# One joint inversion for both streams, mixers without GpSimd, and longer runs of part-array products in a two-layer hybrid transformer

## The chip, the core and the metric

The kernel runs on one core of a Trainium2 chip. The metric is the device time of one execution in microseconds (us), the median of the runs shown. The core has a matrix engine (TensorE, in the profile PE; its weight loads are PEld), two engines for elementwise work (VectorE, DVE; ScalarE, ACT), GpSimd (POOL), and SyncE (SP), which issues every transfer here. TensorE writes to PSUM, eight banks of 128 x 512 fp32; all else lies in SBUF.

## The reference

Two layers over two streams of 256 tokens of width 1024: the context `c` and the image `x`. Each layer has a mixer with three branches (a gated delta rule with 8 heads in two directions, a chunk MLP, a pooling branch), then an expert layer of 16 experts in which each expert chooses its tokens. In the second layer the context gives only its states.

```python
def gated_delta_chunked(q, k, v, g, beta, s0):
    ...
    m = jnp.where(strict, jnp.einsum('nbhik,nbhjk->nbhij', kb, kc) * decay, 0.0)
    a = m + jnp.eye(C, dtype=m.dtype)
    rhs = jnp.concatenate([vc * bc[..., None], kb * jnp.exp(gc)[..., None]], axis=-1)
    sol = lax.linalg.triangular_solve(a, rhs, left_side=True, lower=True, unit_diagonal=True)
    ...
    def step(s, xs):
        v_new = u_ - jnp.einsum('bhck,bhkv->bhcv', w_, s)
        o_ = (jnp.einsum('bhck,bhkv->bhcv', q_ * jnp.exp(g_)[..., None], s)
              + jnp.einsum('bhij,bhjv->bhiv', at_, v_new))
        ...
        s = (s * jnp.exp(g_last)[..., None]
             + jnp.einsum('bhck,bhcv->bhkv', k_ * jnp.exp(g_last - g_)[..., None], v_new))
...
for l in range(DEPTH):
    ctx_mix, ctx_states = hybrid_mixer(hc, zero_states, 1, lp, states_only=last)
    x_mix, _ = hybrid_mixer(hx, ctx_states, ROWS, lp, states_only=False)
    x = x + g1x * x_mix
    ...
    x = x + g2x * expert_choice_ffn(hx2, lp)
    ...
```

## The kernel before

The program is recorded first and ordered later. `Net` writes down each operation through `Prog.record`; `Prog.order` is a list scheduler with a cost for each operation (`Prog.cost`) that picks, engine by engine, the next operation by priority (the place where it was recorded, plus a bias) among those whose inputs are ready; `Prog.emit` then issues that fixed order, so every instruction of the profile has the line L623. `s.any`, `s.av`, `s.vg` and `s.ad` stand for operations that the scheduler may give to one of several engines.

Projections multiply in split single precision: each weight tile is cut into a high and a low part (`wsplit`: a ScalarE copy, then a subtraction), and each product is three fp32r products. The gated delta rule works on 128-token chunks, two per stream, and two heads at a time (`j` counts the four head pairs). For each stream and head pair `heads_in` projects, convolves and normalizes keys, values and queries; `heads_solve` makes the triangular matrices `MT` (two chunks x two directions x two heads = 8 of 128 x 128) from transferred rows of decays and calls `inverse`; `heads_scan` carries the state through the chunks; `heads_out` normalizes and gates. The other branches (`side`: `chunk_mlp`, `pooling`, gates) are a generator from which `gdn` takes pieces between these steps; what is left runs behind them. Then come `merge` (branches joined, output projection), `route` (which expert takes which token) and `moe`, in which 16 x 12 tiles of 1 MB of expert weights are loaded for each layer.

`inverse` inverts the 32 x 32 diagonal blocks in four doubling levels. A level is a set of 32 x 32 products into bank `P`, a masked copy `Pn` by VectorE (two halves), a second set into bank `Qm`, an addition and a 32 x 32 block transpose by VectorE. Two more steps join blocks to 64 (`P32`, `Y32`) and to 128 (`P64`, `Y64`). There are 64 small instructions in a set (8 matrices x 4 blocks, each fp32 product being two instructions). One call for each stream and head pair: 8 calls in a layer.

In `Prog.order` ready 32 x 32 products (`op.tile`) wait in a queue of their own beside that of all other TensorE work. The scheduler stays with the small ones only while they write the same bank and the count is no multiple of `quad=12`:

```python
if ready[e] and (x < ready[e][0] and not much or ops[x[1]].a[0].tile is group[0] and group[1] % s.limits["quad"]):
    queues.reverse()
```

In the mixers GpSimd takes the elementwise products of `heads_solve` (`E`, `Eb`, `qt`), the decay of the state in `heads_scan`, most of `heads_out`, the weighting in `heads_z`, parts of `chunk_mlp`, and, where the scheduler chooses it, subtractions and additions of `wsplit`, `split_x`, `side` and `merge`.

Of the kernel before, what the change touches and what calls it, by code (L numbers as in the profile page):

```python
# [5 lines left out]
F32 = mybir.dt.float32  # L6
# [96 lines left out]
def _layouts(inp):  # L103
# [14 lines left out]
    o["gnw"] = f(g["gdn_norm_w"])  # L118
# [103 lines left out]
class Op:  # L222
    __slots__ = ("i", "eng", "fn", "a", "k", "tiles", "deps", "succ", "nd", "cost", "ready", "start", "end", "on", "prio", "gate", "inst", "win", "tile", "fill")
# [34 lines left out]
class Prog:  # L258
    def __init__(s, nc, pool, banks, limits):
# [6 lines left out]
        s.any = Eng(s, ("act", "dve", "pool"))  # L266
        s.av, s.vg = Eng(s, ("act", "dve")), Eng(s, ("dve", "pool"))
# [13 lines left out]
    def record(s, eng, fn, a, k):  # L281
# [47 lines left out]
        op.tile, op.fill = False, 1.0  # L329
# [6 lines left out]
    def cost(s, op, acc):  # L336
# [16 lines left out]
        if op.eng[0] == "pe":  # L353
            if op.fn == "transpose":
                return {"pe": n * 2 / 2.4 + 2}
            m = acc[0][0].shape[0]
            op.fill = min(m, 128) * acc[1][0].shape[0] / 16384
# [15 lines left out]
    def order(s):  # L373
# [110 lines left out]
        recent, group = [], [None, 0]  # L484
# [21 lines left out]
        while left:  # L506
# [17 lines left out]
            for e in engines:  # L524
# [3 lines left out]
                if e == "pe":  # L528
# [3 lines left out]
                    if ready["tile"]:  # L532
# [5 lines left out]
                        if ready[e] and (x < ready[e][0] and not much or ops[x[1]].a[0].tile is group[0] and group[1] % s.limits["quad"]):  # L538
                            queues.reverse()
                aside, tries = [], 0  # L540
                while queues:
# [26 lines left out]
                    if e == "pe":  # L568
                        if not span[3]:
                            c *= 2  # L570
                        if group[0] is not None and not op.tile:
                            c += 80.0
                        group[1] = group[1] + 1 if op.tile and op.a[0].tile is group[0] else 1
                        group[0] = op.a[0].tile if op.tile else None
                        span[1] += c * op.fill
                        span[2] += c
                        if not op.tile:
                            recent.append((now, c * op.fill))
# [52 lines left out]
POOLW = (0, 6)  # L631
# [5 lines left out]
FILL = (3, 1, 1)  # L637
ROOM = dict(w=0, wa=0)
EVERY = (0.7, 1.0)
NY = 3  # L640
# [12 lines left out]
class Net:  # L653
# [43 lines left out]
    def run(s):  # L697
        tc, t = s.tc, s.t
        limits = dict(w=4, hi=5, wa=5, we=18, fill=0.94, window=800, spare=0, clock=4096 / 1.2, share=0.5, quad=12, room=ROOM)
# [9 lines left out]
    def record(s):  # L709
# [28 lines left out]
        for n, sh in (("n1", [128, 2, 8]), ("conv", [128, 2, 24, 5]), ("psc", [128, 2, 4]), ("wr", [128, 2, 8, 16]),  # L738
                      ("alog", [128, 2, 16]), ("dtb", [128, 2, 16]), ("gnw", [128, 2, 128])):
# [15 lines left out]
        for n in ("conv", "psc", "wr"):  # L755
            nc.sync.dma_start(s.small[n], t[n])
        for n, w in (("alog", 16), ("dtb", 16), ("gnw", 128)):
# [59 lines left out]
    def ada(s, l, parts):  # L817

        nc, t = s.nc, s.t
        for g, halves in parts:  # L820
            ps = s.bank("ada")
            js = [j for a in halves for j in (2 * a, 2 * a + 1)]
            for kt in range(8):
                ws = {}
                for a in halves:
                    w = s.p.tile([128, 2, 512], F32, name="wada", lim="wa")
                    nc.sync.dma_start(w.rearrange("p a b -> p (a b)"), t["w_ada"][l, g, a, kt])
                    ws[a] = w
                if kt == 0:
# [4 lines left out]
                for j in js:  # L834
                    s.mm(ps[32 * j:32 * j + 32, :], s.cs32[:, kt, :], ws[j // 2][:, j % 2, :], False, kt == 7)
# [60 lines left out]
    def wsplit(s, src):  # L896
# [14 lines left out]
        s.tt(lo, w, hi.bitcast(F32), ALU.subtract, s.p.vg if s.wn > POOLW[s.l] else nc.gpsimd)  # L911
# [52 lines left out]
    def gdn(s, l, ms, side):  # L964
        p = s.p
        Y, X = [], []
        for r in range(NY):
            Y.append(p.tile([128, 2, 2, 2, 128], F32, name="Y"))
            s.nc.gpsimd.memset(Y[r], 0.0)
            X.append(p.tile([128, 2, 2, 64], F32, name="X64"))  # L970
            s.nc.gpsimd.memset(X[r], 0.0)
        c, x = ms
        slot = lambda m, j: (Y[(2 * j + m.k) % NY], X[(2 * j + m.k) % NY])
        full = [m for m in ms if m.full]
        qkv, sol, zs = {}, {}, {}
# [13 lines left out]
        for m in ms:  # L989
# [857 lines left out]
```

## Time and profile before

| what | value |
|---|---|
| time, median of 3 runs | 2430.93 us (2430.82 to 2431.25) |
| time of the profiled execution | 2433.34 us |
| its span, first to last instruction | 2431.6 us |
| mean granted TensorE clock | 0.961 |
| TensorE, VectorE, ScalarE, GpSimd busy | 2118.4, 1172.9, 647.9, 370.6 us |
| moved from HBM | 597.58 MB |

The span falls into two mixers (to about 883 us, and from 1338 to about 1970 us) and two expert stages behind them. "Busy" counts an instruction from its start to its modelled end, and those of TensorE overlap, so the pace of TensorE is better read from how many instructions a stretch holds. A stretch counts every instruction that touches it, those of its neighbours at both ends too.

### The profile page before, as it was taken

The numbers are of one execution on the slowest core, as the hardware profiler recorded it, in microseconds if no ns is written. First come the engines' busy times: TensorE is split into PE (matmuls) and PEld (weight loads), VectorE is DVE, ScalarE is ACT, GpSimd is POOL, SyncE is SP. The second block draws the span as 40 slices with busy tenths as digits, with TensorE's granted clock in tenths as the row PEclk, the third lists the DMA queues.
The fourth block names the chain that finished last, engine by engine and source line by source line (L and its number), as shares of the span: only waits on it lengthen the run. The fifth ranks groups of instructions, "written<-read, shape, count | busy, mean of one in ns | idle before, by whom it ended". The sixth has DMA issues, their size and how long they took to land.

```text
span 2431.6 us, 50016 instructions
## 1 busy us (share of the span) xinstructions
PE 2118.4 (87%) x21357; PEld 1351.6 (56%) x21357; DVE 1172.9 (48%) x2712; ACT 647.9 (27%) x1329; POOL 370.6 (15%) x334
## 2 busy tenths in 40 slices
PE   8999999999999999878787899999899977676665
PEld 4777867787779842222222477777789931111211
DVE  4978776854326831212121797788765531010102
ACT  4534343323224520000000454344434420000000
POOL 0233332510000410000000212232330010000000
PEclk9999999999999999999999999999899988888888
DMA  8432333323346689999999634333236879999997
GB/s 291 146 101 82 117 90 99 99 102 101 118 162 203 214 320 421 421 421 421 421 421 421 243 113 152 128 118 122 69 101 217 317 315 421 421 421 421 422 421 307
DMA packets 153910, 603.11 MB, mean 248 GB/s; under 512 B 13820, under 2 KB 60092, under 8 KB 104536
## 3 DMA queue, kind: packets, MB, share of 16 engines
q1 hardware_dynamic: 153688, 599.93, 64.9%
q8 instruction: 167, 2.74, 0.4%
q14 instruction: 55, 0.45, 0.1%
HBM read 597.58 MB, written 2.29 MB: 247 GB/s over the span
## 4 chain that ended last, share of the span: by engine, by line
PE 45%; DMA 36%; DVE 12%; issue 3%; POOL 2%; ACT 1%; SPq 0%; DVEq 0%; ACTq 0%; POOLq 0%
PE bank L623 45%; DMA page<-in_w_up_dram 22%; DVE page L623 12%; DMA page<-in_w_down_dram 12%; POOL page L623 2%; ACT page L623 1%; DMA page<-in_w_gate_dram 0%; DMA page<-in_n_dram 0%; DMA page<-in_b_ada_dram 0%; DMA page<-rows 0%; SPq L623 0%; DMA page<-in_w_ada_dram 0%; DVEq L1843 0%; DVEq L623 0%; POOLq L623 0%
## 5 line engine op out<-in xcount | busy, mean ns | idle before, releaser
L623 PE MATMUL bank<-page,page 32*32 32x32 f32 (+8 forms) x18473 | 2074.4, 335 | 299.6 <-DVE page L623 107.3
L623 PEld LDWEIGHTS bank<-page,page 128*128 128x128 f32 (+5 forms) x18473 | 1300.2, 144 | 1048.4 <-issue 381.3
L623 POOL TENSOR_TENSOR page<-page,page 128x512 f32<-128x512 f32 (+4 forms) x277 | 313.5, 1146 | 1444.1 <-DVE page L623 1050.3
L623 ACT ACTIVATE page<-page 128x1024 fp32r<-128x1024 f32 (+8 forms) x462 | 326.5, 721 | 534.2 <-PE bank L623 273.6
L623 ACT ACTIVATE page<-bank 128x512 f32<-128x512 f32 (+5 forms) x341 | 164.9, 501 | 1106.9 <-PE bank L623 1012.1
L623 DVE TENSOR_TENSOR page<-page,page 128x1024 fp32r<-128x1024 f32 (+6 forms) x389 | 338.5, 888 | 118.9 <-ACT page L623 102.0
L623 DVE TENSOR_TENSOR page<-page,bank 128x256 f32<-128x256 f32 (+2 forms) x184 | 101.4, 558 | 575.9 <-ACT page L623 269.1
L623 DVE TENSOR_TENSOR page<-bank,page 128x128 f32<-128x128 f32 (+4 forms) x350 | 154.5, 460 | 287.2 <-PE bank L623 282.6
L623 ACT ACTIVATE page<-page,page 128x128 f32<-128x128 f32 (+2 forms) x319 | 119.9, 435 | 50.2 <-POOL page L623 31.2
L623 DVE COPY page<-bank 32x128 f32<-32x128 f32 (+7 forms) x175 | 71.4, 408 | 60.9 <-PE bank L623 58.9
L623 DVE SCALAR_TENSOR_TENSOR page<-page,page,page 128x508 f32<-128x508 f32 (+3 forms) x128 | 94.5, 757 | 1.2
L623 DVE SCALAR_TENSOR_TENSOR page<-page,page 128x508 f32<-128x508 f32 (+5 forms) x115 | 75.9, 665 | 14.1 <-DMA page<-in_n_dram 11.7
L623 PE MATMUL bank<-page 32*32 32x32 f32 (+1 forms) x2884 | 76.2, 204 | 2.8 <-DVE page L623 2.4
L623 PEld LDWEIGHTS bank<-page 32*32 32x32 f32 (+1 forms) x2884 | 59.2, 114 | 20.0 <-issue 8.5
L623 POOL MEMSET page<- 128x1024 f32 (+2 forms) x13 | 7.6, 630 | 398.6 <-DMA page<-in_w_up_dram 389.7
L623 DVE TENSOR_SCALAR page<-page 128x4 f32<-128x4 f32 (+7 forms) x215 | 52.6, 258 | 26.2 <-ACT page L623 19.2
L623 DVE STREAM_TRANSPOSE page<-page 32x32 f32<-32x32 f32 (+1 forms) x208 | 57.8, 288 | 4.2
L623 DVE SCALAR_TENSOR_TENSOR page<-page,bank 128x512 f32<-128x512 f32 x48 | 32.7, 684 | 55.9 <-PE bank L623 54.7
L623 ACT ACTIVATE page<-bank,page 128x128 f32<-128x128 f32 (+2 forms) x81 | 36.7, 483 | 78.5 <-PE bank L623 60.0
L623 DVE TENSOR_TENSOR page<-page 128x4 f32<-128x4 f32 (+3 forms) x252 | 50.5, 209 | 4.1
L623 POOL TENSOR_TENSOR page<-page 128x512 f32<-128x512 f32 x22 | 30.9, 1406 | 138.7 <-DVE page L623 96.1
L623 DVE TENSOR_SCALAR page<-page,page 128x128 f32<-128x128 f32 (+3 forms) x125 | 47.4, 416 | 5.2 <-ACT page L623 4.8
(25 smaller groups left out, 235.5 us busy)
## 6 DMA issues: line engine op xcount, KB each, us to landing
page<-in_w_gate_dram SPq DMA_DIRECT2D x128, 1024.0 KB, 19.8
page<-in_w_up_dram SPq DMA_DIRECT2D x128, 1024.0 KB, 19.8
page<-in_w_down_dram SPq DMA_DIRECT2D x128, 1024.0 KB, 19.8
page<-in_w_in_dram SPq DMA_DIRECT2D x136, 512.0 KB, 3.6
page<-in_w_ada_dram SPq DMA_DIRECT2D x96, 512.0 KB, 4.6
page<-rows SPq DMA_DIRECT2D x88, 256.0 KB, 5.0
page<-in_w_br_a_dram SPq DMA_DIRECT2D x24, 512.0 KB, 4.7
page<-in_w_out_dram SPq DMA_DIRECT2D x24, 512.0 KB, 4.6
```

The lines of the kernel that those rows point to most:

```text
L623: op.inst = getattr(eng[op.on], fn)(*a, **k)
```

## The change

- **Joint inversion.** `heads_solve` now takes both streams: `products` fills the `MT` of each (two tiles, one for each direction, of 8 matrices), and one call of `inverse` handles all 16. A set has 128 small instructions in a full bank; VectorE works on 512 columns at once instead of 256, with one masked copy instead of two halves. 4 calls in a layer. Two slots for the results instead of three; the order in `gdn` and the pieces taken (`FILL`) follow.
- **No GpSimd in the mixers.** Its operations go to VectorE, some to ScalarE (squares with accumulation in `heads_out`; the state's decay to either). Two products of `heads_out` become one instruction for each head, and the norm weight moves into the ScalarE copy behind the transposes. `route`, `final` and the zeroing of buffers keep GpSimd.
- **Longer runs.** Every product with at most 64 rows or columns (`op.part`) waits in the small queue, those of the experts and of `ada` too, and once the scheduler has begun with one it stays until none is ready. Its prices change with it. `ada` issues the products of two weight tiles together.

```diff
@@ Prog.cost
-            op.tile = m <= 32 and acc[1][0].shape[0] <= 32
+            op.tile = m <= 32 and k <= 32
+            op.part = m <= 64 or k <= 64
             if acc[2][0].dtype == F32R and n >= 256:
-                return {"pe": n / 2.4 + 2}
-            c = max(n, m) / 1.2 * 2 + 4
-            return {"pe": c if m > 64 else c * (0.6 if m > 32 else 0.25) + 20 if n < 128 else c * (0.5 if m > 32 else 0.25) + 14}
+                return {"pe": n / 2.4 + 13.5}
+            c = n / 0.6 + 10
+            if op.tile:
+                return {"pe": 9.0}
+            if op.part:
+                return {"pe": max(c / (4 if m <= 32 or k <= 32 else 2) + 6, 30)}
+            return {"pe": max(c, 223)}
@@ Prog.order
-                        heapq.heappush(ready["tile" if op.tile else e], (op.prio, op.i))
+                        heapq.heappush(ready["tile" if op.part else e], (op.prio, op.i))
...
-                        if ready[e] and (x < ready[e][0] and not much or ops[x[1]].a[0].tile is group[0] and group[1] % s.limits["quad"]):
+                        if ready[e] and (x < ready[e][0] and not much or group[2]):
                             queues.reverse()
...
-                        if group[0] is not None and not op.tile:
-                            c += 80.0
+                        if group[2] and not op.part:
+                            c += 225.0
+                        elif op.part and not group[2]:
+                            c += 95.0
+                        group[2] = op.part
...
-POOLW = (0, 6)
-FILL = (3, 1, 1)
-NY = 3
+FILL = (6, 1, 2)
+NY = 2
@@ ada
-            for kt in range(8):
+            for k2 in range(4):
...
+                for kt in (2 * k2, 2 * k2 + 1):
+                    for j in js:
+                        s.mm(ps[32 * j:32 * j + 32, :], s.cs32[:, kt, :], ws[kt, j // 2][:, j % 2, :], False, kt == 7)
@@ wsplit
-        s.tt(lo, w, hi.bitcast(F32), ALU.subtract, s.p.vg if s.wn > POOLW[s.l] else nc.gpsimd)
+        s.tt(lo, w, hi.bitcast(F32), ALU.subtract)
@@ gdn
-        for m in ms:
-            sol[m.k] = s.heads_solve(m, 0, qkv[0][m.k], slot(m, 0))
-            take(FILL[0])
+        sol = s.heads_solve(ms, 0, qkv[0], Y[0], X[0])
+        take(FILL[0])
...
-                o[m.k], S = s.heads_scan(m, j, qkv[j][m.k], sol[m.k], S)
+                o[m.k], S = s.heads_scan(m, j, qkv[j][m.k], now[m.k], S)
                 take(FILL[1])
-                if j < 3:
-                    sol[m.k] = s.heads_solve(m, j + 1, qkv[j + 1][m.k], slot(m, j + 1))
+                if j < 3 and m is ms[0]:
+                    sol = s.heads_solve(ms, j + 1, qkv[j + 1], Y[(j + 1) % NY], X[(j + 1) % NY])
                     take(FILL[2])
@@ heads_solve
+    def heads_solve(s, ms, j, qkv, Y, XF):
+        MT = [s.p.tile([128, 8, 128], F32, name="MT") for d in range(2)]
+        part = {m.k: s.products(m, j, qkv[m.k], [a[:, 4 * z:4 * z + 4, :] for a in MT]) for z, m in enumerate(ms)}
+        s.inverse(MT, Y, XF)
+        return {m.k: (Y[:, :, 4 * z:4 * z + 4, :],) + part[m.k] for z, m in enumerate(ms)}
+    def products(s, m, j, qkv, MT):
...
-            s.tt(E, R[0], s.nb[:, :, None, :].to_broadcast(B4), ALU.add, G)
+            s.tt(E, R[0], s.nb[:, :, None, :].to_broadcast(B4), ALU.add)
...
-            s.tt(Eb, E, R[2], ALU.mult, G)
-            s.tt(MT[:, i], kq[:, 0][:, None].to_broadcast(B4), Eb, ALU.mult)
+            s.tt(Eb, E, R[2], ALU.mult)
+            for d in range(2):
+                s.tt(MT[d][:, 2 * i:2 * i + 2, :], kq[:, 0], Eb[:, d], ALU.mult)
...
@@ heads_scan
-                    s.tt(sd[:, d], S[:, d], col(i, 5)[:, d, :, None].to_broadcast([128, 2, 128]), ALU.mult, G)
+                    for h in range(2):
+                        s.p.ad.scale(sd[:, d, h, :], S[:, d, h, :], col(i, 5)[:, d, h:h + 1])
@@ heads_out
-        s.tt(osq, o, o, ALU.mult, G)
-        V.reduce_sum(so, osq, axis=AX.X)
+                s.act(s.p.tile([128, 128], F32, name="osq"), o[:, i, h, :], AF.Square, accum_out=so[:, i, h:h + 1])
...
-        s.tt(o, o, ro[:, :, :, None].to_broadcast(B4), ALU.mult, G)
-        s.tt(o, o, zs, ALU.mult, G)
+                V.scalar_tensor_tensor(o[:, i, h, :], o[:, i, h, :], ro[:, i, h:h + 1], zs[:, i, h, :], op0=ALU.mult, op1=ALU.mult)
...
@@ inverse
-        C5 = [128, 2, 2, 2, 32]
+        C4 = [128, 2, 8, 32]
...
-            for (i, d, h) in units:
+            for (d, u) in units:
                 for q in range(4):
-                    s.mm(pp[Q[q], i, d, h, :], MT[Q[q], i, d, h, 32 * q:32 * q + 32], X[Q[q], i, d, h, :], True, True)
-            for i in range(2):
-                s.tt(Pn[:, i], pp[:, i], s.nm[:, lv, :, None, :].to_broadcast([128, 2, 2, 32]), ALU.mult)
+                    s.mm(pp[Q[q], d, u, :], MT[d][Q[q], u, 32 * q:32 * q + 32], X[Q[q], d, u, :], True, True)
+            s.tt(Pn, pp, s.nm[:, lv, :, None, :].to_broadcast(C4), ALU.mult)
...
-        for i in range(2):
-            for h in range(2):
-                V.transpose(XF[Q[1], i, h, 0:32], Y[Q[0], i, 0, h, 32:64])
-                V.transpose(XF[Q[2], i, h, 32:64], Y[Q[3], i, 1, h, 64:96])
+        V.transpose(line(XF[Q[1], 0]), line(yc[Q[0]]))
+        V.transpose(line(XF[Q[2], 1]), line(yc[Q[3]]))
...
@@ merge
-            s.tt(x[:, :, cs], x[:, :, cs], tm, ALU.add, s.p.vg if c < 3 else V)
+            s.tt(x[:, :, cs], x[:, :, cs], tm, ALU.add)
```

## Rows read from the trace of the kernel before

**Rows 1.** The page, busy us (share of the span) and instructions of each engine.
```profile
PE 2118.4 (87%) x21357; PEld 1351.6 (56%) x21357; DVE 1172.9 (48%) x2712; ACT 647.9 (27%) x1329; POOL 370.6 (15%) x334
```

**Rows 2.** Windows by stage: length, busy PE, PEld, DVE, ACT, POOL, clock, DMA share, GB/s.
```profile
90.00:510.00 420.00, 395.10 (x6649) 315.34 (x6649) 318.32 (x817) 163.09 (x383) 148.15 (x136) 0.98 0.32 99
510.00:780.00 270.00, 269.88 (x1614) 217.58 (x1600) 117.24 (x180) 84.10 (x114) 16.36 (x15) 1.00 0.40 135
...
883.00:1338.00 455.00, 388.06 (x1634) 121.60 (x1632) 81.58 (x119) 12.99 (x20) 6.43 (x9) 1.00 1.01 416
1338.00:1440.00 102.00, 91.83 (x579) 59.59 (x580) 83.25 (x220) 51.68 (x119) 23.22 (x14) 0.95 0.55 196
1440.00:1797.00 357.00, 330.23 (x6288) 263.10 (x6287) 280.94 (x751) 155.76 (x365) 112.81 (x110) 0.97 0.37 116
1797.00:1925.00 128.00, 128.00 (x1110) 126.99 (x1109) 77.58 (x106) 53.45 (x63) 5.59 (x4) 1.00 0.62 207
...
1970.00:2431.60 461.60, 309.01 (x2157) 90.26 (x2155) 62.45 (x130) 15.65 (x28) 4.98 (x4) 0.87 0.97 402
```

**Rows 3.** The chain that ended last, in order of time: start us, us, what.
```profile
516.35 263.47 PE bank L623 x1436
...
998.75 19.81 DMA page<-in_w_down_dram
```

**Rows 4.** Windows of TensorE alone: length, busy PE (instructions that touch it), clock, DMA.
```profile
108.19:108.87 0.68, 0.68 (x64) 1.00 0.00 0
...
242.07:242.62 0.55, 0.55 (x49) 1.00 0.90 209
242.62:243.17 0.55, 0.55 (x11) 1.00 0.78 276
243.17:243.43 0.26, 0.26 (x18) 1.00 0.91 331
1840.00:1860.00 20.00, 20.00 (x169) 1.00 0.64 192
1802.17:1802.78 0.61, 0.61 (x17) 1.00 0.11 27
```

**Rows 5.** Lines by form of TensorE, 242.08 to 242.61 and 242.63 to 243.16 us.
```profile
L623 PE MATMUL bank<-page,page 32*32 32x32 f32 x48 | 0.6, 195 | 0.0
...
L623 PE MATMUL bank<-page,page 128*128 128x256 f32 x3 | 0.6, 314 | 0.0
```

**Rows 6.** Lines by form of TensorE, 90 to 880 and 1340 to 1965 us: its 32 x 32 products.
```profile
L623 PE MATMUL bank<-page,page 32*32 32x32 f32 x3328 | 46.3, 196 | 13.5 <-DVE page L623 8.2 <-issue 5.1
L623 PE MATMUL bank<-page 32*32 32x32 f32 x1280 | 19.0, 197 | 2.8 <-DVE page L623 2.4 <-issue 0.4
...
L623 PE MATMUL bank<-page,page 32*32 32x32 f32 x3200 | 45.9, 196 | 15.2 <-DVE page L623 9.3 <-issue 5.9
```

**Rows 7.** Lines by form of GpSimd and VectorE: whole span, then 1880 to 1920 and 90 to 510 us.
```profile
L623 POOL TENSOR_TENSOR page<-page,page 128x512 f32<-128x512 f32 x144 | 196.1, 1372 | 1145.3 <-DVE page L623 924.3 <-PE bank L623 81.3 <-DMA page<-rows 79.5
L623 DVE TENSOR_TENSOR page<-page,page 128x512 f32<-128x512 f32 x33 | 23.3, 706 | 1.0
L623 DVE TENSOR_TENSOR page<-bank,page 128x512 f32<-128x512 f32 x74 | 49.5, 685 | 30.9 <-PE bank L623 29.0 <-POOL page L623 0.9 <-ACT page L623 0.4
L623 DVE TENSOR_TENSOR page<-bank,page 128x128 f32<-128x128 f32 x128 | 31.4, 283 | 30.1 <-PE bank L623 29.9
L623 DVE TENSOR_TENSOR page<-page,bank 128x256 f32<-128x256 f32 x88 | 35.8, 417 | 62.3 <-PE bank L623 62.1
L623 DVE STREAM_TRANSPOSE page<-page 128x256 f32<-128x256 f32 x80 | 35.2, 440 | 1.2
...
L623 DVE TENSOR_TENSOR page<-page,page 128x1024 fp32r<-128x1024 f32 x13 | 15.7, 1221 | 3.3 <-ACT page L623 3.3
L623 DVE TENSOR_TENSOR page<-page,page 128x1024 fp32r<-128x1024 f32 x31 | 41.8, 1351 | 7.2 <-ACT page L623 6.8
```

**Rows 8.** The chain that ended last, 780 to 890 us: shares of the stretch by line.
```profile
by line: PE bank L623 47.8%; DVE page L623 25.4%; DMA page<-in_n_dram 7.4%; POOL page L623 7.2%; issue 6.7%; DMA page<-in_w_ada_dram 4.1%; ACT page L623 1.6%; DVEq L623 0.1%; POOLq L623 0.1%
```

More of the change, by code (lines that the diff above doesn't have):

```diff
@@ L222 @@
 class Op:
-    __slots__ = ("i", "eng", "fn", "a", "k", "tiles", "deps", "succ", "nd", "cost", "ready", "start", "end", "on", "prio", "gate", "inst", "win", "tile", "fill")
+    __slots__ = ("i", "eng", "fn", "a", "k", "tiles", "deps", "succ", "nd", "cost", "ready", "start", "end", "on", "prio", "gate", "inst", "win", "tile", "part", "fill")
 class Eng:
@@ L328, in record @@
             op.win = 10 ** 9
-        op.tile, op.fill = False, 1.0
+        op.tile, op.part, op.fill = False, False, 1.0
         op.cost = s.cost(op, shapes)
@@ L698, in run @@
         tc, t = s.tc, s.t
-        limits = dict(w=4, hi=5, wa=5, we=18, fill=0.94, window=800, spare=0, clock=4096 / 1.2, share=0.5, quad=12, room=ROOM)
+        limits = dict(w=4, hi=5, wa=5, we=18, fill=0.94, window=800, spare=0, clock=4096 / 1.2, share=0.5, room=ROOM)
         with tc.tile_pool(name="sb", bufs=1) as sb, tc.tile_pool(name="ps", bufs=1, space=PSUM) as ps, \
@@ L1272, in heads_scan @@
         nc, k, full, cl = s.nc, m.k, m.full, m.cl
-        V, G = nc.vector, nc.gpsimd
+        V = nc.vector
         B4 = [128, 2, 2, 128]
@@ L1363, in heads_out @@
         s.rsqrt(ro, so, [2, 2])
-        s.tt(o, o, ro[:, :, :, None].to_broadcast(B4), ALU.mult, G)
-        s.tt(o, o, zs, ALU.mult, G)
+        for i in range(2):
+            for h in range(2):
+                V.scalar_tensor_tensor(o[:, i, h, :], o[:, i, h, :], ro[:, i, h:h + 1], zs[:, i, h, :], op0=ALU.mult, op1=ALU.mult)
         yp = s.bank("yp").rearrange("p (h c) -> p h c", h=2)
@@ L1384, in inverse, with c4 @@
-        units = [(i, d, h) for i in range(2) for d in range(2) for h in range(2)]
-        YT = s.p.tile(C5, F32, name="Yc")
+        flat = lambda a: a.rearrange("p d u c -> p (d u c)")
+        units = [(d, u) for d in range(2) for u in range(8)]
+        def c4(name):
+            return s.bank(name).rearrange("p (d u c) -> p d u c", d=2, u=8)
+        YT = s.p.tile(C4, F32, name="Yc")
         for q in range(4):
             for d in range(2):
-                s.tt(YT[Q[q], :, d], MT[Q[q], :, d, :, 32 * q:32 * q + 32],
-                     s.nm[Q[q], 0, 1 - d, None, None, :].to_broadcast([32, 2, 2, 32]), ALU.mult, s.p.vg)
@@ L1411, in inverse @@
+            V.transpose(flat(YT), flat(X))
         for q in range(4):
-            for d in range(2):
-                s.p.any.copy(Y[Q[q], :, d, :, 32 * q:32 * q + 32], YT[Q[q], :, d, :, :])
-        s.p.any.copy(XF[Q[0], :, :, 0:32], X[Q[0], :, 0])
-        s.p.any.copy(XF[Q[1], :, :, 32:64], X[Q[1], :, 0])
-        s.p.any.copy(XF[Q[2], :, :, 0:32], X[Q[2], :, 1])
-        s.p.any.copy(XF[Q[3], :, :, 32:64], X[Q[3], :, 1])
-        th = [(i, h) for i in range(2) for h in range(2)]
-        c3 = lambda name, w: s.bank(name)[:, 0:4 * w].rearrange("p (t h c) -> p t h c", t=2, h=2)
+            s.p.av.copy(units16(Y)[Q[q], :, 32 * q:32 * q + 32], units16(YT)[Q[q]])
@@ L1421, in inverse @@
+        for q in range(4):
+            s.p.av.copy(XF[Q[q], q % 2], X[Q[q], q // 2])
+        c3 = lambda name, w: s.bank(name)[:, 0:8 * w].rearrange("p (u c) -> p u c", u=8)
         pp = c3("P32", 32)
-        for (i, h) in th:
+        for u in range(8):
             for a, b in ((0, 1), (2, 3)):
-                s.mm(pp[Q[b], i, h, :], MT[Q[a], i, 0, h, 32 * b:32 * b + 32], X[Q[a], i, 0, h, :], True, True)
-                s.mm(pp[Q[a], i, h, :], MT[Q[b], i, 1, h, 32 * a:32 * a + 32], X[Q[b], i, 1, h, :], True, True)
```

148 lines of the change are left out of this document (71 added, 77 removed).

## The prediction, made before the changed kernel was run

> **What bounds the kernel now.** I read the page's busy times first, then windows cut by stage, then the chain that ended last, then short windows inside the inversions. The page puts TensorE at 87% of the span [rows 1], but that is an average over stages of two kinds. In the two expert stages DMA is at its limit: 416 GB/s with a DMA share of 1.01 from 883 to 1338 us, and 402 GB/s in the last 462 us [rows 2], where the chain goes from transfer to transfer at 19.8 us a step [rows 3]. The change moves no byte of these, and TensorE has 67 of 455 us free in the first of them, so they only start earlier or later. What can move is the mixers. There TensorE is busy 395 of 420 and 330 of 357 us while the gated delta rule runs, and without a gap in the stretches behind it (270 and 128 us), when only side branches are left [rows 2, 3]. With work left over at the end, a mixer's length is TensorE's own time plus its gaps, not the latency of an inversion. So each edit is priced by what it takes from TensorE's issue or adds to its gaps.
>
> **What a change of shape costs TensorE.** In the windows, a run of 48 small (32 x 32) instructions takes 0.55 us to the start of the next wide one, a run of 16 takes 0.26 us (the counts beside them hold one and two wide ones still in flight) [rows 4, 5]. The slope is 0.29/32 = 0.009 us for each, and 0.55 - 48 x 0.009 = 0.115 us is left for going in and out. Between them stand 3 products of 128 x 256, in 0.55 us [rows 4, 5]; undisturbed, 168 of them take 20 us (a count of 169 with one in flight), 0.119 us each [rows 4], so 0.55 - 0.36 = 0.19 us is lost on the wide side. One excursion costs 0.115 + 0.19 = 0.31 us, whatever its length.
>
> **How many there are.** Read in this way, the inversions make 291 runs of small products in the two mixers (142 and 149), the first at 108.19 us with 64 instructions, the last at 1802.17 us [rows 4]. By the code 16 calls with 12 sets each are 192; the rest are sets cut at 24 products (48 instructions) by the limit of 12, as in 48 + 16 above.
>
> **The change part by part.**
>
> *Joint inversion and longer runs.* The products are the same in number: 4608 small instructions in the first mixer [rows 6], 128 in a set now instead of 64, at the same 0.009 us. Only excursions go. Eight calls with 12 uncut sets are 96 runs, 195 fewer: 195 x 0.31 = 60 us. The least I can argue for is what half of it would be, each joint set broken in two by a late operand: 192 runs, 99 fewer, 31 us. The most adds other part products that join an inversion's run; I put 10 us on that, some 30 more excursions.
>
> *`ada` in pairs.* 32 steps become 16 pairs, 16 excursions fewer, 16 x 0.31 = 5 us at most, 0 if the queue had joined them already; I take 4.
>
> *Gaps at the hand-overs.* TensorE stands idle 13.5 + 2.8 + 15.2 = 31.5 us before small products [rows 6]. There are half as many hand-overs now, each longer: a level's VectorE work for two calls was 2 x (2 x 0.283 + 0.417 + 0.440) = 2.8 us, and is about 0.685 + 0.685 + 0.7 = 2.1 us in one (the transpose of 512 columns estimated from that of 256 and the ratio 685 to 417) [rows 7]. But two calls could cover one another before. Halved gaps would be -16 us, all of them gone -31 us, doubled gaps +31 us. I take 0, in the middle, and keep both ends.
>
> *GpSimd's work to VectorE.* A 128 x 512 product takes GpSimd 1.37 us and VectorE 0.71 us [rows 7], a ratio of 0.51. In the two stages with inversions GpSimd's 148 and 113 us thus become at most 76 and 58 us; some vanish (norm weight, one of two passes in `heads_out`) or go to ScalarE, which is busy 163 of 420 us [rows 2]. Against that stand 0.77 us saved at each of 16 levels in a mixer, 12 us. VectorE also loses time when GpSimd works beside it: its subtraction of 128 x 1024 averages 1.35 us between 90 and 510 us, and 1.22 us where GpSimd stands still [rows 7], 4 us for 31 of them, and other forms with two SBUF inputs should gain in the same way. VectorE then has at most 318 + 76 - 12 - 4 = 378 of 420 and 281 + 58 - 12 = 327 of 357 us. That is under the bound, and wide products cover what waits, so I charge TensorE nothing. Without that cover it would cost what VectorE exceeds its stage by, priced below.
>
> *Latencies with no cover.* From 780 to 890 us, where the branches merge and tokens are routed, the chain runs over GpSimd for 7.2% of 110 us, 8 us [rows 8]. At the ratio above most of it falls to half: 4 us gained. At the start of a layer the joint call must wait for both streams' matrices, and from 1338 to 1440 us VectorE is already busy 83 of 102 us with 23 us of GpSimd's work to come [rows 2], 12 us at the ratio. TensorE has projections to do there. Value taken 0, bound 12 us lost.
>
> *Nothing for the rest.* Two slots instead of three, the small load of the norm weight and the zeroed buffers are hidden behind projections. Expert products in the small queue may run ahead of transposes, but DMA sets that stage's pace and 67 us of TensorE are free in it [rows 2].
>
> **The sum.** -60 - 4 - 4 = -68 us. The profiled execution took 2433.3 us, 2.4 us over the median of the runs, so 2433.3 - 68 = 2365.3 us for it, and 2430.9 - 68 = 2363 us as a median.
>
> **A rule that speaks against it.** The granted clock is 0.98 and 0.97 in the two stages with inversions [rows 2]; at two levels, 2.4 and 1.2 GHz, that is 2 x (0.02 x 420 + 0.03 x 357) = 38 us at the lower one. The stages behind them, nearly without small products, stand at 1.00 [rows 2]. The Trainium skill, in "TensorE: Matmul & The Clock Gate", section "What's actually happening", says that the throttled state is the default and that the matrix engine's activity releases it. By that rule longer runs that fill a sixteenth of the array could lower the clock more often; by the rows the present runs cost little. It becomes a rival below.
>
> **The rivals.**
> 1. *The runs fall by half only.* Joint sets break where a bank or operand is late. For it: sets are cut already. Against it: one masked copy now frees a whole set at once. 2430.9 - 31 - 4 - 4 = 2392 us.
> 2. *The joint call is not covered (slower).* One chain instead of two that interleave: VectorE's part of it is about 4 x 2.1 us in the levels and, estimated from the same rows, 11 us around them, 20 us a call, 160 us for 8. Today 31.5 us of hand-overs are bare. The gain of 68 us is gone when 100 of the 160 us are bare, 62%; at 75% it is 120 - 31.5 - 68 = +20, 2451 us. Against it: the wide work left behind both stages, 270 and 128 us [rows 2], is available as cover.
> 3. *VectorE becomes the bound (slower).* If GpSimd's work took as long on VectorE as before, it would need 318 + 148 = 466 of 420 and 281 + 113 = 394 of 357 us, 83 us too much: 2430.9 - 68 + 83 = 2446 us. The ratio of 0.51 speaks against it.
> 4. *The clock falls more often.* Twice the 38 us at the lower level, half of them lost: +19, 2382 us.
>
> **How the numbers follow.** Forecast 0.62, rival 1 0.17, rival 2 0.11, rival 3 0.05, rival 4 0.05. The predicted time is 2363 us. The forecast's own range takes the bounds of its unknown terms: -31 and -10 below, 2322; +31 above, 2394. To hold 8 in 10 it must reach beyond rival 1 with some of its gaps, and towards the slower cases without holding them: 2318 to 2425 us. Faster by over 0.2% (4.9 us, about what a measurement of this kernel can tell from no change) 0.82; within 0.2% 0.04, from the passage between rivals 1 and 2; slower 0.14.
>
> **What would show it.** Right: wide and small runs alternate about 100 times in the two mixers for the inversions, with runs of 128; the stages behind them keep TensorE without a gap; the expert stages keep their 455 us and start earlier by what the mixers lost; idle time before small products stays near 31 us; VectorE's 128 x 1024 subtraction falls to 1.22 us everywhere; GpSimd is idle in the mixers. Wrong: idle before small products over 100 us (rival 2), VectorE above 95% in the stages with inversions (rival 3), a granted clock under 0.95 there (rival 4), or some 190 runs (rival 1). It would also be wrong if the new prices in the scheduler moved the wide work itself, which I priced at nothing.

## The result, and the profile after

The changed kernel takes 2394.73 us (median of 4 runs, 2393.57 to 2398.76) against 2431.07 us for the kernel before on the same chip: a ratio of 0.985, with a 95% interval of 0.984 to 0.987. That is 36 us faster, where 68 us were forecast, and inside the range of 2318 to 2425 us. The profiled execution took 2393.84 us. Its page, with each engine's busy time in us (share of the span) and number of instructions:

```profile
span 2392.1 us, 49338 instructions
PE 2041.2 (85%) x21357; PEld 1344.3 (56%) x21357; DVE 1122.6 (47%) x2478; ACT 686.3 (29%) x1466; POOL 49.3 (2%) x41
```

TensorE has the same 21357 instructions as in [rows 1] and is busy 77 us less. GpSimd's 370.6 us are down to 49.3, and VectorE, which took most of that work over, is busy *less* than before: 1122.6 us against 1172.9. The windows by stage of the changed kernel (length, busy PE, PEld, DVE, ACT, POOL, clock, DMA share, GB/s):

```profile
90.00:497.00 407.00, 369.91 (x6813) 309.33 (x6811) 302.67 (x733) 180.54 (x437) 0.00 (x0) 0.97 0.31 97
497.00:757.00 260.00, 259.51 (x1444) 219.24 (x1443) 110.93 (x170) 86.71 (x128) 0.00 (x0) 1.00 0.44 149
...
866.00:1317.00 451.00, 385.36 (x1636) 123.03 (x1636) 82.73 (x120) 12.99 (x20) 8.64 (x8) 1.00 1.01 418
...
1420.00:1754.00 334.00, 290.19 (x6334) 250.69 (x6320) 238.33 (x558) 159.91 (x398) 0.00 (x0) 0.93 0.32 102
1754.00:1908.00 154.00, 154.00 (x1292) 153.84 (x1291) 96.44 (x146) 70.53 (x104) 0.00 (x0) 1.00 0.69 237
```

Against [rows 2]: the first expert stage keeps its pace at a DMA share of 1.01, and the side stages stay without a gap. But the stages with inversions have 37 and 44 us without TensorE at work, where the kernel before had 25 and 27, and the granted clock is 0.97 and 0.93 there, where it was 0.98 and 0.97. The last expert load of each layer leaves 20.5 and 38.5 us earlier (1307.8 and 2355.0 us against 1328.3 and 2393.5), so each mixer gave about 20 us, where some 34 were expected. The 32 x 32 products by form, 90 to 860 us and then 1318 to 1945 us (busy us, mean ns of one | idle before them, and what ended it):

```profile
L628 PE MATMUL bank<-page,page 32*32 32x32 f32 x4416 | 53.8, 200 | 24.4 <-issue 24.0 <-DVE page L628 0.3
L628 PE MATMUL bank<-page 32*32 32x32 f32 x192 | 2.3, 194 | 1.2 <-issue 1.2
...
L628 PE MATMUL bank<-page,page 32*32 32x32 f32 x4224 | 50.6, 200 | 23.7 <-issue 22.9 <-DVE page L628 0.7
L628 PE MATMUL bank<-page 32*32 32x32 f32 x384 | 4.8, 208 | 0.5 <-issue 0.5
```

The sum, 49.8 us, stands against 31.5 us in [rows 6]. More telling is the releaser: before it was mostly VectorE, now it is "issue", time in which TensorE waits for nothing that the profile shows. TensorE's timeline at 228 us (start, length, what, [idle before]) shows where these gaps lie, and the DMA view of 225 to 262 us what else goes on:

```profile
227.81 2.43 PE L628 MATMUL bank<-page,page 32*32 32x32 f32 x94
231.09 2.74 PE L628 MATMUL bank<-page,page 32*32 32x32 f32 x128 [0.85 <-issue]
235.10 1.97 PE L628 MATMUL bank<-page,page 32*32 32x32 f32 x50 [1.26 <-issue]
236.99 0.87 PE L628 MATMUL bank<-page 32*32 32x32 f32 x78
239.10 0.64 PE L628 MATMUL bank<-page 32*32 32x32 f32 x50 [1.24 <-issue]
```
```profile
GB/s 0 0 0 0 186 337 62 0 18 0 0 0 18 0 0 0 18 0 0 0 18 0 0 0 97 257 221 9 18 0 0 18 0 0 0 18 0 0 0 0
...
q8 instruction: 9, 0.15, 1.6%
```

The gaps stand in the middle of a burst, 0.85 to 1.26 us each. Between the larger transfers, a small one comes every 3 to 4 us (the lone 18s of the GB/s line): the instruction queue, with 9 packets of 16 KB in 37 us. Over the whole span it moves 167 of them, for 2 x 21357 matmuls and weight loads: 256 instructions a packet. A joint set of 64 products is 128 matmuls and 128 weight loads, 256 instructions in some 1.2 us.

In the table below, *runs* are TensorE's runs of products on part of the array in the two mixers (those of `ada` and of other small work too, so 361 where the prediction counted 291 of the inversions alone), *inside* is its idle time within stretches of 32 x 32 products, and *idle* all its idle time from 85 us to the first expert products of each layer, all summed from the trace's matmuls in order.

### The profile page after: what moved, and what is told of

Its sections match the earlier page's. It is cut to its first block, busy times and chain, and to the rows that moved or that the text cites. A ratio compares the mean times of both kernels' runs of the same rounds, so it can differ in the third digit from the quotient of the medians.

```text
span 2392.1 us, 49338 instructions
## 1 busy us (share of the span) xinstructions
PE 2041.2 (85%) x21357; PEld 1344.3 (56%) x21357; DVE 1122.6 (47%) x2478; ACT 686.3 (29%) x1466; POOL 49.3 (2%) x41
## 4 chain that ended last, share of the span: by engine, by line
PE 49%; DMA 36%; DVE 9%; issue 4%; ACT 2%; SPq 0%; DVEq 0%; ACTq 0%
PE bank L628 49%; DMA page<-in_w_up_dram 19%; DMA page<-in_w_down_dram 10%; DVE page L628 9%; DMA page<-in_w_gate_dram 3%; ACT page L628 2%; DMA page<-in_w_in_dram 1%; DMA page<-rows 1%; DMA page<-in_w_ada_dram 1%; DMA page<-in_n_dram 0%; SPq L628 0%; DMA page<-in_b_ada_dram 0%; ACT L628 0%; DVEq L1849 0%; DVEq L628 0%
## 5 line engine op out<-in xcount | busy, mean ns | idle before, releaser
L628 PE MATMUL bank<-page,page 32*32 32x32 f32 (+8 forms) x20611 | 2024.4, 322 | 338.0 <-DVE page L628 99.0
L628 PEld LDWEIGHTS bank<-page,page 32*32 32x32 f32 (+5 forms) x20611 | 1321.4, 143 | 1031.5 <-issue 398.8
L628 ACT ACTIVATE page<-page 128x1024 fp32r<-128x1024 f32 (+7 forms) x485 | 341.4, 719 | 499.3 <-PE bank L628 244.7
L628 DVE TENSOR_TENSOR page<-page,page 128x1024 fp32r<-128x1024 f32 (+3 forms) x471 | 401.5, 876 | 151.7 <-ACT page L628 128.4
L628 DVE TENSOR_TENSOR page<-page,bank 128x512 f32<-128x512 f32 (+2 forms) x152 | 96.6, 644 | 578.8 <-ACT page L628 265.7
L628 DVE TENSOR_TENSOR page<-bank,page 128x512 f32<-128x512 f32 (+4 forms) x286 | 147.7, 530 | 283.8 <-PE bank L628 280.5
L628 ACT ACTIVATE page<-page,page 128x128 f32<-128x128 f32 (+2 forms) x388 | 143.9, 435 | 48.4 <-DVE page L628 41.0
L628 DVE SCALAR_TENSOR_TENSOR page<-page,page,page 128x508 f32<-128x508 f32 (+4 forms) x188 | 107.8, 595 | 1.2
L628 DVE COPY page<-bank 128x512 f32<-128x512 f32 (+7 forms) x100 | 52.6, 527 | 36.9 <-PE bank L628 35.4
L628 DVE SCALAR_TENSOR_TENSOR page<-page,page 128x512 f32<-128x512 f32 (+5 forms) x93 | 65.2, 706 | 9.5 <-DMA page<-in_n_dram 7.4
L628 ACT ACTIVATE page<-bank,page 128x256 f32<-128x256 f32 (+2 forms) x85 | 42.0, 516 | 83.3 <-PE bank L628 64.7
```

Of the source, the lines that this page charges most:

```text
L628: op.inst = getattr(eng[op.on], fn)(*a, **k)
```

## The experiments

Every ratio is to the kernel before on the same chip.

| kernel | us | ratio, 95% interval | runs | inside, us | idle, us |
|---|---|---|---|---|---|
| before | 2431.1 | | 361 | 11.0 | 85.4 |
| changed | 2394.7 | 0.985 (0.984 to 0.987) | 139 | 46.9 | 117.1 |
| x1_cut32 | 2401.8 | 0.989 (0.987 to 0.991) | 198 | 25.9 | 95.6 |
| b1_newqueue | 2444.6 | 1.004 (1.002 to 1.006) | 231 | 21.9 | 125.8 |
| a1_oldqueue | 2411.3 | 0.991 (0.989 to 0.993) | 288 | 8.5 | 83.9 |
| x2_space20 | 2387.8 | 0.982 (0.980 to 0.983) | 126 | 22.5 | 114.9 |
| c1_fill92 | 2437.1 | 1.002 (1.000 to 1.003) | 131 | 47.0 | 143.9 |
| c2_fill95 | 2403.5 | 0.989 (0.987 to 0.991) | 135 | 42.9 | 120.0 |
| g1_gpsimd | 2443.2 | 1.004 (1.003 to 1.006) | 140 | 46.4 | 145.6 |
| g2_sameorder | 2426.0 | 0.997 (0.996 to 0.999) | 139 | 40.7 | 129.2 |
| t1_two | 2383.5 | 0.980 (0.978 to 0.982) | 235 | 28.1 | 85.9 |
| t3_two_fill90 | 2393.5 | 0.984 (0.982 to 0.987) | 231 | 25.2 | 84.8 |
| t2_two_space12 | 2354.3 | 0.968 (0.965 to 0.970) | 218 | 7.4 | 69.7 |

**1. Bursts alone (m1_bursts).** No planner and no other engine.

```
for n in (16, 32, 48, 64, 96, 128, 256):
    for _ in range(12):
        small(n, mt, xx, 32)   # n f32 products 32x32x32: 2n matmuls
        wide(48)               # 128x256
...
for gap in (3, 6, 12, 24):
    for _ in range(12):
        small(64, mt, xx, 32)
        wide(gap)
...
for n in (64, 128, 256):
    for _ in range(12):
        small(n, bt, bx, 32)   # bf16: n matmuls
        wide(48)
```

> A kernel that computes nothing of the reference: TensorE alone, bursts of n products of 32 x 32 x 32 on constant data, with 48 wide products of 128 x 256 between two bursts, no wait on any other engine, 12 bursts of each n = 16 to 256, then bursts of 64 with 3 to 24 wide products between them, then bursts in bf16 (half as many instructions for a product), then 64 products with 128 columns each. Theory of supply (TensorE's instructions arrive in packets of 16 KB, 256 instructions, and a burst of small products uses them up faster than they come): bursts of 16 and 32 products have hardly a gap, bursts of 64 (256 instructions with their weight loads) have one gap of 1.0 to 1.5 us nearly each, 128 two and 256 about four, so 12, 24 and 48 us or so of idle time in the 12 bursts; bf16 bursts of 128 behave like those of 64 in f32. Rival (the gaps come from the other engines' work, late operands or the scheduler): no idle time in any burst, 64 products in 1.2 us everywhere.

Measured (1749 us in all): the 32 x 32 products by form, in this order: bursts of 16 to 64, of 96, of 128, of 256; bursts of 64 behind 6, 12 and 24 wide products; bf16 bursts of 64 and 128, and of 256; bursts of 64 with 128 columns. Then the timeline of one burst of 256.

```profile
L693 PE MATMUL bank<-xx,mt 32*32 32x32 f32 x3840 | 42.2, 193 | 0.0
L693 PE MATMUL bank<-xx,mt 32*32 32x32 f32 x2304 | 23.3, 194 | 11.0 <-issue 11.0
L693 PE MATMUL bank<-xx,mt 32*32 32x32 f32 x3072 | 32.4, 198 | 22.3 <-issue 22.2
L693 PE MATMUL bank<-xx,mt 32*32 32x32 f32 x6144 | 73.7, 210 | 70.6 <-issue 70.6
...
L693 PE MATMUL bank<-xx,mt 32*32 32x32 f32 x1536 | 20.9, 211 | 9.6 <-issue 9.4
L693 PE MATMUL bank<-xx,mt 32*32 32x32 f32 x1536 | 17.6, 194 | 8.9 <-issue 8.9
L693 PE MATMUL bank<-xx,mt 32*32 32x32 f32 x1536 | 15.8, 193 | 2.1 <-issue 2.1
...
L693 PE MATMUL bank<-bx,bt 32*32 32x32 bf16 x2304 | 22.0, 177 | 0.0
L693 PE MATMUL bank<-bx,bt 32*32 32x32 bf16 x3072 | 28.8, 179 | 25.8 <-issue 25.8
L693 PE MATMUL bank<-xl,mt 32*32 32x128 f32 x1536 | 44.4, 268 | 0.0
```
```profile
812.77 1.50 PE L693 MATMUL bank<-xx,mt 32*32 32x32 f32 x155
816.32 1.27 PE L693 MATMUL bank<-xx,mt 32*32 32x32 f32 x128 [2.04 <-issue]
819.79 1.92 PE L693 MATMUL bank<-xx,mt 32*32 32x32 f32 x128 [2.20 <-issue]
823.26 1.60 PE L693 MATMUL bank<-xx,mt 32*32 32x32 f32 x101 [1.55 <-issue]
```

The gaps are there with every other engine still, so the rival falls. They lie exactly 128 matmuls apart, one packet of 256 instructions, and the next 128 start 3.47 us later (816.32 to 819.79). The DMA records of the traces tie them to the packets: each of the 96 gaps over 0.3 us here ends 1.19 to 1.60 us after a packet of the instruction queue has landed, and so do all 41 between small products of the changed kernel (1.20 to 1.57 us), which make up 46.1 of its 46.9 us inside the runs. They go by instructions: 128 products in bf16, one matmul each, behave like 64 in f32 (no gap), and 256 like 128 (25.8 and 22.3 us). The expectation was wrong on two points: a burst of 64 behind a pause of 48 wide products has no gap, and bursts of 256 lose 70.6 us, not 48. A burst of 64 stalls only when it follows soon on another: 9.6 us in 12 bursts behind 6 wide products, 2.1 us behind 24. In the changed kernel's planned order 56 of 71 pauses between long runs are under 12 wide products.

The Trainium skill, "Runtime: NRT & Kernel Launch", section "Instruction fetch mechanics", says that instructions are fetched in blocks of 16 KiB, 256 of them, and that the cost of crossing a block is mostly hidden. The traces agree on the block, not on the cost: 134.5 + 25.8 us of 1747 here are idle time inside such bursts.

**2. The parts of the change on their own (x1_cut32, b1_newqueue, a1_oldqueue).** The first keeps the changed kernel's order and moves some wide products into the middle of a set; the others swap the queue rule and the prices with it.

```
x1  -        for op in out:
    +        for op in s.cut(out, 32, 12, 4):   # cut a set once, where no operand or bank stands against it
b1  (before) - ... or ops[x[1]].a[0].tile is group[0] and group[1] % s.limits["quad"]):
             + ... or group[2]):                # and the new prices; separate inversions, GpSimd as before
a1  (changed) the same lines the other way round, old prices
```

> The changed kernel with its own planned order, in which only 53 of the uncut sets of 64 small products are cut once after 32, by moving some 4 wide products from behind the set into the middle; 59 more excursions of TensorE (190 to 249 runs of part-array products in the order of its instructions). Theory of supply: the idle time inside runs of 32 x 32 products, 50 us in the changed kernel, falls to 10 to 20 us, the excursions cost 59 x 0.31 = 18 us, so 10 to 22 us faster than the changed kernel, 2373 to 2385 us. Rival (the gaps belong to the hand-overs of the joint call, whatever the run's length): gaps stay near 50 us, the excursions cost 18 us, 2413 us.

> The kernel before with the new queue rule and the new prices of TensorE alone: separate inversions of 32 products a set, uncut, GpSimd and the loads as before. By the order of its instructions 283 runs of part-array products against 419 before and 190 in the changed kernel. Prediction's price: 136 x 0.31 = 42 us less than before, 2389 us, if the gaps stay. Theory of supply: they do stay (12 us inside the runs), since 32 products are half a packet, so 2385 to 2395 us and no slower than the changed kernel. Rival (the joint call is what pays): no more than 20 us gained, 2411 us or above. Second rival (the new prices alone move the wide work for the worse): not faster than before.

> The changed kernel with the queue rule and the prices of before (small products held together for 12, then by priority): joint inversion and no GpSimd stay. By the order of its instructions 346 runs against 419 before and 190 in the changed kernel, none of them over 67 products, most under 48. Price of the excursions: 73 x 0.31 = 23 us under before, 2408 us. Theory of supply: idle time inside the small runs falls from 50 to under 30 us, so 2390 to 2405 us. Rival (joint hand-overs are bare and the long runs cover nothing): total stalls of TensorE stay at 160 us or rise, 2415 us or above.

In x1, the time inside the runs fell by 21 us, to 26, not to 10 to 20; 59 more runs at 0.31 us cost 18, and the two cancel: its profiled span is 2392.4 us against 2392.1, its median 7 us more. Neither the gain of 10 us nor the rival's loss of 18 came. The old queue (a1) took 2411 us, near its price of 2408 and a little above the theory's range, with 8.5 us inside the runs. b1 surprised, though its second rival had named the outcome: 130 runs fewer than before and yet 0.4% slower. Its idle time is 40 us up, 25 of them waits for VectorE and most of the rest "issue", which eats the 130 x 0.31 = 40 us that the runs save. With GpSimd in place the new queue and its prices, swapped together here, gain nothing in the one order that was tried.

**3. A pause for the instructions (x2_space20), and GpSimd or separate inversions with a control (c1_fill92, g1_gpsimd, t1_two).**

```
x2  -  if ready[e] and (x < ready[e][0] and not much or group[2]):
    +  if ready[e] and (group[0] >= 20 and x < ready[e][0] and not much or group[2]):
       ...
    +  group[0] = 0 if op.part else group[0] + 1
c1  -  fill=0.94
    +  fill=0.92
g1  =  c1 and, for instance
    -  s.tt(Eb, E, R[2], ALU.mult)
    +  s.tt(Eb, E, R[2], ALU.mult, nc.gpsimd)
t1  =  c1 and
    -  if j < 3 and m is ms[0]:
    -      sol = s.heads_solve(ms, j + 1, ...)
    +  if j < 3:
    +      sol.update(one(m, j + 1))      # sets of 32 products, NY = 3, FILL = (3, 1, 1)
```

> The changed kernel with one more condition in the queue rule: after a run of part-array products at least 20 wide products go first, where any are ready, before the next run. In the changed kernel's planned order 56 of the 71 pauses between two long runs of small products are under 12 wide products, mostly 5; here 15 of 70, and 49 are 20 or more. 173 runs instead of 190. Theory of supply (in the kernel that only makes bursts, pauses of 6 to 12 wide products left stalls of 0.5 to 1.8 us in nearly every burst of 64, pauses of 24 in 2 of 12): idle time inside the small runs falls from 47 us to under 15, excursions save 17 x 0.31 = 5 us, 2355 to 2370 us. Rival (the inversion's chain sets the mixer's length, so a pause put into it is paid): the gain inside the runs is lost as idle time behind them, 2390 us or above.

> A control for the next two: the changed kernel with the scheduler allowed 92% of SBUF instead of 94%, nothing else. It measures what a reshuffled order alone does to the time: 2385 to 2405 us if the order of the rest matters little; outside of that, differences of the next two below that size say nothing.

> The control (92%) with GpSimd's work in the mixers given back: the decay matrices, the scaled queries and states, the norm's scale and bias, the mixed product, and the choice between VectorE and GpSimd where before had it; the norm weight's pass stays out. Joint inversion and new queue stay. The prediction charged this move nothing on TensorE, and 4 us at the merge: within 8 us of the control, 4 us slower as the middle. Rival (VectorE and GpSimd hinder each other and GpSimd's latency feeds TensorE late): 15 us or more slower than the control, and TensorE waits for GpSimd in it. Second rival (VectorE was loaded to the point where TensorE waits for it): faster than the control.

> The control (92%) with the inversion of each stream by itself again (three buffers, sets of 32 products), GpSimd idle and the new queue kept. By the order of its instructions 287 runs of part-array products against 183 of the control. The prediction's price: 104 x 0.31 = 32 us slower than the control. Theory of supply adds that the runs of 32 products stall less, so 10 to 20 us slower only. The kernel before with the new queue alone took 2444 us, 0.4% over before, so a third outcome, 2430 us and above, would say that the new queue without the joint call leaves hand-overs bare.

x2 halved the time inside the runs (46.9 to 22.5 us), but most came back as waits for VectorE: 7 us gained, not 25 to 40. Both theories hold in part: the pause takes stalls away, and the joint inversion's chain pays for it in waits. The control, c1, tells most: two hundredths less room for the planner cost 42 us, with nearly the same number of runs (131 and 139) and the same time inside them. TensorE's waits for VectorE and ScalarE grew, and its clock in 90 to 497 us fell to 0.93. So g1, 6 us over its control, says little, and t1, 54 us under it and 11 us under the changed kernel, contradicts the price of 32 us *for* the joint call.

**4. GpSimd's work back in the same order; the luck of the order; the pause with separate inversions.**

```
g2  -  s.tt(Eb, E, R[2], ALU.mult)              # for instance
    +  s.tt(Eb, E, R[2], ALU.mult, s.nc.back)   # planned for VectorE, marked op.pool
       ...
    -  op.inst = getattr(eng[op.on], fn)(*a, **k)
    +  op.inst = getattr(eng["pool" if op.pool else op.on], fn)(*a, **k)
c2  =  changed kernel, fill=0.95
t3  =  t1, fill=0.90
t2  =  t1 and x2's condition with 12 for 20
```

> The changed kernel in its own planned order, instruction for instruction, in which 112 of VectorE's operations in the mixers are issued on GpSimd instead, as before had them (decay matrices and their masked copies, scaled queries, the norm's scale and bias, the mixed product); every other engine's order is that of the changed kernel, so that nothing is reshuffled. If the prediction's charge of nothing for this move is right: within 8 us of the changed kernel, 2387 to 2403 us. Rival (GpSimd's longer instructions feed TensorE late and slow VectorE beside them, so the move itself gained a good part of the time): 15 us or more slower, TensorE waiting for GpSimd.

> The changed kernel with the scheduler allowed 95% of SBUF instead of 94%. With 92% it took 42 us more, with no change in the number of its runs. If the room in SBUF sets that time: 2395 us or less here. If it is only the luck of the order that the greedy scheduler comes to: anywhere from 2385 to 2440 us, so 2410 us or above would show it.

> The kernel with separate inversions, no GpSimd and the new queue (2383 us at 92% of SBUF), with at least 12 wide products after a run of part-array products before the next, where any are ready. Pauses between two long runs rise from mostly 3 to 5 wide products to 12, runs fall from 287 to 266. Theory of supply: a set of 32 products uses half a packet, and 12 wide products are the pause of 24 for 64 that left hardly a stall in the kernel of bursts, so idle time inside the runs falls from 28 us to under 12, excursions save 21 x 0.31 = 6 us: 2355 to 2370 us. Rival (the time put into the inversion's chain comes back as idle time at the hand-overs): 2380 us or above.

> The kernel with separate inversions, no GpSimd and the new queue once more, with 90% of SBUF instead of 92%: another order of the same work. If separate inversions stand up to less room because their tiles are half as large: 2380 to 2395 us. If the 2383 us at 92% was luck of the order: 2400 us or above. Together with the three orders of the joint call (92%, 94%, 95%) it tells whether the joint call itself gained anything over separate ones under the new queue, for which the prediction had 32 us.

g2 is the cleanest answer on GpSimd: 106 operations by the page (GpSimd's count goes from 41 to 147) moved back, nothing reordered, 31 us lost of the 36 that the change had gained. The page of g2 and its windows with inversions, then its VectorE's 128 x 128 scalings from 90 to 497 us; below them the same row of the changed kernel:

```profile
PE 2060.7 (85%) x21357; PEld 1355.7 (56%) x21357; DVE 1123.3 (46%) x2372; ACT 688.5 (28%) x1466; POOL 198.2 (8%) x147
...
90.00:497.00 407.00, 360.20 (x6714) 300.59 (x6713) 286.13 (x649) 175.12 (x423) 76.29 (x56) 0.94 0.31 95
...
1444.00:1778.00 334.00, 290.62 (x6191) 250.23 (x6192) 240.50 (x510) 154.41 (x382) 51.71 (x36) 0.91 0.32 103
```
```profile
L629 DVE TENSOR_SCALAR page<-page,page 128x128 f32<-128x128 f32 x58 | 28.0, 514 | 7.8 <-POOL page L629 6.5 <-PE bank L629 1.2
```
```profile
L628 DVE TENSOR_SCALAR page<-page,page 128x128 f32<-128x128 f32 x58 | 14.5, 280 | 1.3 <-PE bank L628 1.2
```

VectorE gave up 106 instructions of some 0.69 us each and is busy as long as with them (1123.3 and 1122.6 us): most of the 73 us came back as longer instructions beside GpSimd, 514 ns instead of 280 for these. That mean hides two kinds: 44 of the 58 took 271 to 299 ns as in the changed kernel, and 13 took 1.27 to 1.36 us, near the 1.41 us of GpSimd's own 128 x 512 products. This agrees with the Trainium skill, "SBUF — State Buffer", section "Who interferes with whom", by which VectorE and GpSimd share a pair of ports, and in some of VectorE's modes, which `tensor_scalar` can enter, whichever issues first holds the pair for its whole instruction while the other blocks. The rival had also expected TensorE to wait for GpSimd; in g2 it is never seen to. The loss shows as 12 us more idle time in the mixers and as a lower clock (0.94 and 0.91 against 0.97 and 0.93). One reservation: the planner had priced these operations as VectorE's, so an order planned for GpSimd might lose less. b1 beside t1 and t3 points the same way, separate inversions under the new queue with GpSimd (1.004) and without it (0.980 and 0.984), though these differ in `ada`, in the code of the inversion and in SBUF room as well.

c2, at 2404 us, lies between its limits and settles only that the order alone spreads the joint kernel over 2395 to 2437 us. t3 stayed low: 2384 and 2394 us for two orders of the separate one. t2 did what the theory of supply said, 2354 us, 40 us faster than the changed kernel and 77 us faster than before. Its 32 x 32 products by form, 90 to 860 and 1318 to 1945 us, and its windows with inversions:

```profile
L629 PE MATMUL bank<-page,page 32*32 32x32 f32 x3232 | 39.6, 194 | 1.8 <-DVE page L629 1.5 <-issue 0.3
L629 PE MATMUL bank<-page 32*32 32x32 f32 x1376 | 16.5, 194 | 0.9 <-DVE page L629 0.5 <-issue 0.4
...
L629 PE MATMUL bank<-page,page 32*32 32x32 f32 x3008 | 37.5, 195 | 4.6 <-issue 3.2 <-DVE page L629 1.3
L629 PE MATMUL bank<-page 32*32 32x32 f32 x1600 | 19.4, 194 | 2.9 <-issue 2.9
```
```profile
90.00:480.00 390.00, 378.41 (x6722) 313.81 (x6723) 315.41 (x848) 188.86 (x470) 0.00 (x0) 0.99 0.33 104
...
1400.00:1720.00 320.00, 299.87 (x6093) 256.58 (x6092) 268.32 (x722) 177.04 (x443) 0.00 (x0) 0.98 0.39 126
```

"Issue" before small products is down from 48.6 to 6.8 us, and the clock stands at 0.99 and 0.98. Of the 29 us that t2 gained over t1, 20.7 are idle time inside the runs and 5 the 17 runs fewer; but only one order of it was run, so how much of the gain is luck of the order is not known.

## Why the prediction was right, and where it was not

The sign, the range and the sum's first term held. Two terms that were taken as nothing did not, the gaps and GpSimd's work, and the joint inversion did not earn what it was given.

*The excursions* fell as priced, a little further: 361 runs to 139 in the mixers, 222 x 0.31 = 69 us, for the 64 of the first two terms. Counted as the prediction did, for the inversions alone, 102 are left where 96 were expected, 64 of them with 100 small instructions or more. The 0.31 us also fit the experiments: before's time less 0.31 us a run plus the change in idle time gives 2394, 2388, 2407 and 2390 us for the changed kernel, x2, a1 and t3, which took 2395, 2388, 2411 and 2394. It is no law: the three kernels that keep GpSimd's work or part of it beside the new queue (b1, g1, g2) took 13 to 20 us more than it gives, c1 19, x1 11 and c2 8, and t1 and t2 9 and 17 less.

*Gaps at the hand-overs, taken as 0 between -31 and +31,* is the step that failed. Idle time of TensorE in the mixers rose by 31.7 us (85.4 to 117.1), just over the upper bound, and 69 - 32 = 37 us is what the change gained. Before 32 x 32 products alone, where the prediction read the term, it rose by 18 us (31.5 to 49.8). Its nature was missed too. The prediction looked for operands that come late from VectorE; inside the bursts it rose by 35.9 us, where 256 instructions in 1.2 us outrun a supply of one packet in 3.5 us, and everywhere else it fell by 4.2. m1 shows the mechanism, the packets' landings show it in the changed kernel itself, and t2 shows that it can be taken away.

*The joint inversion* earned nothing here that separate ones do not earn under the new queue: it saves some 100 runs against t1 and t3 (31 us) and has 31 to 59 us more idle time. Three orders of it took 2395, 2404 and 2437 us, two of the separate one 2384 and 2394.

*GpSimd's work, charged as nothing,* was mis-sized in the other direction. The bounds on VectorE were right (303 of 407 us and 238 of 334, under the 378 and 327 allowed), and its 128 x 1024 subtraction does take 1.22 us in both stages. But the 4 us for what GpSimd costs VectorE beside it were far too little: giving the work back costs 31 us (g2). These 31 us are no further term of the sum, since 69 - 32 makes up the whole gain without them; with b1 they suggest that the saved excursions reach the kernel's time only with GpSimd out of the way.

*The clock.* At the two levels, 2.4 and 1.2 GHz, the windows with inversions stood at the lower one for 38 us before (the prediction's sum) and, by the same sum, 2 x (0.03 x 407 + 0.07 x 334) = 71 us in the changed kernel, 109 in g2, 110 in c1 (0.93 and 0.92) and 21 in t2. If half of that is lost, an estimate, g2 loses 19 us to it over the changed kernel, which with its 12 us of idle time makes the 31. c1 and g2 are also 19 and 20 us over what runs and idle time give, and t2 is 17 us under; x2, with 89 us at the lower level and on the mark, does not follow this. So the close fit of 69 - 32 to the gain is in part luck: it leaves out some 16 us for the clock, and what paid them back stays open.

*The rivals.* Rival 1 named 2392 us, almost the measured time, for a reason that is not there: it had 192 runs left for the inversions, and 102 were found. Rival 2 is half true: the joint chain does have less cover, as x2 and c1 show, yet the idle time before small products is 49.8 us and not over 100. Rival 3 is out. Rival 4 is half true as well: its mark, a clock under 0.95, is met in one stage (0.93), and the time at the lower level did nearly double. What lowers the clock was not found. In m1 bursts of 256 bf16 products with gaps ran at 0.82 and bursts of 64 and 128 without gaps at 1.00, but f32 bursts of 64 behind 12 wide products also ran at 1.00, with 8.9 us of gaps.

*Left open:* `ada` in pairs (4 us) and the merge without GpSimd (4 us) were not tried alone. Why one order of the joint kernel is 42 us slower than another is shown only as far as the waits for VectorE and ScalarE and the lower clock; which late operand begins it stays open. And the kernel before was run in one order only: with 42 us between orders of the joint kernel, how much of the 36 us belongs to the order is not known.

## What to carry to other kernels

Count instructions as well as time when many small products are put in a row: a burst may be as long as the fetched instructions last, and after it TensorE needs slow work before the next. Price an engine's removal by what it does to its neighbour, not only by its own busy time. And where a greedy planner orders the work, run several orders before a gain of 1% is given to an edit; an edit made in a fixed order tells far more.

## What the runs showed of the hardware

- A packet of 256 instructions came every 3.47 us during long bursts of small products, while a rested burst used one up in 1.2 us. TensorE went on 1.2 to 1.6 us after the packet had landed. A burst of 128 matmuls and 128 weight loads behind 48 wide products never stalled; one of 192 matmuls did in half the cases, after 147 or more.
- VectorE's 128 x 128 scaling took 280 ns with GpSimd still and 514 ns on average beside it, either as before or some 1.3 us; moving 106 operations to GpSimd freed no time on VectorE.
- With 31 us lost in g2, no wait of TensorE for GpSimd is seen: 12 us are idle time behind other engines, and the granted clock fell from 0.97 and 0.93 to 0.94 and 0.91.
